# Score products of two head groups in row groups of TensorE, and two small products over all rows, in a two-layer hybrid mixer on one core

## The chip, the cores and the metric

The kernel runs on one core of a Trainium2 chip. The metric is the device time of one execution in microseconds (us); the time before is the median of three runs.

## The reference

One inference step of a backbone with two layers. There are 256 context tokens and 1024 latent tokens, 1280 rows of 1024 features. A layer normalises and modulates the tokens, projects them with `w_in` (1024 x 4400), runs three groups of heads side by side, and projects their gated result back with `w_out`:

- A, mLSTM: 4 heads of 128, exponential input gates with a running maximum m as stabiliser, a matrix state per head. The divisor of a token is `max(|den|, exp(-m))`.
- B, retention: 4 heads of 64 with a fixed decay per head, and a rotation of q and k on the latent tokens.
- C, gated linear attention: 4 heads with keys of 32 and values of 64, and a decay per key feature that comes out of a rank-16 product: `log_a = log_sigmoid(clr @ gla_w2 + gla_b2) / 16`.

Every group runs one scan forward and one backward over the tokens and adds the two; context tokens scan only themselves, latent scans start from cached states. In chunk form a group computes, per chunk, `scores = q k^T` times a decay, `scores @ v`, and the product of q with the state at the chunk's edge. The outputs are both normalised token arrays and the final context states.

## The kernel before, in words

Tokens are worked on in 10 chunks of 128 (chunks 0 and 1 are the context). The projections (`mm_fm`, L438, and `mm_tm`, L450) split both operands in two parts and take three products of 24 accumulating matmuls into one of two PSUM banks `pj`; everything else in PSUM goes through a ring `mx` of six banks. SBUF has 12 large tiles `f`, taken and given back, and rings of smaller ones (`rw`, 8 tiles of 512 columns, among them).

The order of the instructions on each engine is not written out. The program states every step, `ORDER` names the order of the steps of a layer, which gives their priority, and a planner that simulates all engines while the program is built lays the instructions of each engine in a row. A projection's matmuls get a priority lower by `LATE` (`late()`, L137), so that they fill what the mixers leave free on TensorE. Once laid, the order is fixed: an instruction that waits holds all behind it on its engine.

The steps that the change touches:

- **Gate rows** (`mlstm_rows`, L539). Forward heads are on partitions 0-3, backward heads on 32-35. A tile `TR` of 128 partitions collects gate rows in four quadrants. Ten transposes of `TR` (L590) and one copy per bank (L591) make the columns `ccol`. The row tile `m` becomes exp(-m) on ScalarE (L585); ten further transposes, of 36 rows (L595), and two copies a bank (L597) make the columns `ecol`.
- **Decays** (`decays`, L621). For each pair p of heads one matmul per block of tokens (L645), with the weights `w2[:, p, :]` on 64 partitions and the gate tile `G[0:64, ...]`.
- **C scores** (`group_c`, L804 to L832). Tiles `q[p]`, `k[p]` hold pair p: forward rows of its two heads on partitions 0-63, backward rows on 64-127, 32 rows per head and direction. For every two chunks GpSimd (L810) and ScalarE (L811) make copies of the queries in which one head of each direction is zeroed, and per chunk four matmuls over 64 rows with 256 columns (L819) put forward scores in one bank and backward scores in another. VectorE masks the forward scores into `PT` (L822) and overwrites the later half with the backward ones (L823). The output bank takes the state product (L827) and four score products (L830), and goes to `head_out` (L603).
- **B scores** (`group_b`, L1026 to L1038). For every two chunks eight matmuls over 64 rows with 128 columns (L1034), the heads on partitions 0-63 into one bank, those on 64-127 into the other; VectorE multiplies by the decay matrices (L1038).

In the trace every matmul in plain float32 (these all are) has two records, each with its weight load; transposes and the projections' matmuls have one.

Of the kernel before, what the change touches and what calls it, by code (L numbers as in the profile page):

```python
# [10 lines left out]
F32 = mybir.dt.float32  # L11
# [4 lines left out]
ALU = mybir.AluOpType  # L16
# [11 lines left out]
# the steps of layer() of either layer, in the order of their priority  # L28
# [11 lines left out]
# columns of w_in  # L40
# [13 lines left out]
def constants():  # L54
# [21 lines left out]
    # two-dimensional axial rotary angles of the latent grid  # L76
# [12 lines left out]
def hybrid_step(ctx: ExitStack, tc: tile.TileContext, A, O):  # L89
# [7 lines left out]
    class Ring:  # L97
        """n fixed tiles, handed out in turn; a tile may be used until its turn comes again"""
# [9 lines left out]
    class Arena:  # L108
        """fixed tiles [P, 1290], taken and given back; the one given back longest ago goes first"""
# [23 lines left out]
    def v3(t, n):  # L133
        """[P, a * n] as [P, a, n]"""
        return t.rearrange("p (a n) -> p a n", n=n)

    def late():  # L137
# [11 lines left out]
    heads_of = cp.tile([P, 2], F32, name="heads_of")  # L149
    for i in range(4):  # L150
        h = slice(32 * i, 32 * i + 32)
        pool.memset(heads_of[h, 0:1], 1.0 - i % 2)
        pool.memset(heads_of[h, 1:2], float(i % 2))
# [6 lines left out]
    # tau, as the decays of both directions take it  # L160
# [8 lines left out]
    # vectors as columns  # L169
# [21 lines left out]
    # half of headnorm_g, for silu through tanh  # L191
# [7 lines left out]
    def log_sigmoid(x, u, w):  # L199
        """x <- log(sigmoid(x)), with log1p(u) = ln(w) - ((w - 1) - u) for w = fl(1 + u); u, w scratch"""  # L200
# [33 lines left out]
    # small per-layer values that live long  # L234
# [12 lines left out]
    # scratch in DRAM  # L247
# [22 lines left out]
    def ada(l, c0, n, t, k):  # L270
        """loads k tiles k .. of n columns of w_ada into t; the tiles as views"""
# [5 lines left out]
    def modulation_pe(l, c0, n, units):  # L277
        """n columns on TensorE, a unit [P, k tiles * n] a step"""
# [15 lines left out]
    def modulation_dve(l, c0, n, acc, units):  # L294
        """n columns on VectorE, a unit [P, k tiles * n] a step; acc: two tiles [P, n]"""
# [24 lines left out]
    def background():  # L320
        """the next of the modulations that later stages need; its end comes with the next call"""
# [29 lines left out]
    def load_x(b):  # L351
        """tokens of block b, over their rms"""
# [26 lines left out]
    def norm_h(l, b, xn):  # L379
        """tokens over their rms, to modulated feature tiles, split"""  # L380
# [20 lines left out]
    # ---------------------------------------------------------------- weights  # L401
# [9 lines left out]
    def w_fm(src, c0):  # L411
        """128 columns of a weight matrix, split, [P, KT, 128]"""
# [1023 lines left out]
```

## Time and profile before

| what | value |
|---|---|
| time, median of 3 runs (lowest, highest) | 1673.07 us (1667.36, 1677.04) |
| span of the profiled execution, first to last instruction | 1660.9 us |
| the profiled execution's own time | not printed apart from its span |
| mean granted clock of TensorE | 0.987 |
| TensorE busy | 1591.4 us (96%) |
| VectorE, ScalarE, GpSimd busy | 1006.1 (61%), 614.1 (37%), 153.2 (9%) us |
| DMA | 167.43 MB, 101 GB/s |

"Busy" of an engine is the time in which at least one of its instructions is under way. PE is TensorE's matmuls, PEld its weight loads, DVE is VectorE, ACT ScalarE, POOL GpSimd, SP the engine whose queue issues most DMAs. The run's median is 12.2 us above the span of the profiled execution.

### The profile page before, as it was taken

What the parts mean: (1) busy time and instruction counts of PE and PEld (TensorE: products, weight loads), DVE (VectorE), ACT (ScalarE), POOL (GpSimd) and SP (SyncE); (2) the same over time, 40 slices, a digit from 0 to 9 for tenths busy, and PEclk for the clock granted to TensorE, in tenths of its full rate; (3) what the DMA queues carried; (4) which work ended last, traced back from release to release, by engine and by line L of the source; (5) the groups of instructions that cost most, each with busy time, mean ns of one, the idle gap of its engine ahead of it and who ended that gap; (6) DMA issues with size and microseconds to landing.
All of it is one profiled execution on the core that took longest, in us unless ns stands there. A gap on an engine that the chain in (4) does not pass through costs nothing.

```text
span 1660.9 us, 28470 instructions
## 1 busy us (share of the span) xinstructions
PE 1591.4 (96%) x10834; PEld 1429.1 (86%) x10834; DVE 1006.1 (61%) x2550; ACT 614.1 (37%) x1603; POOL 153.2 (9%) x242
## 2 busy tenths in 40 slices
PE   5898999999999999999999899999999999999997
PEld 1797879888989998889999787899988989888997
DVE  5766664768679855864364677454537633456545
ACT  2735424434112324342265453244411223434323
POOL 0200121001001101000011012100001100000001
PEclk8999999999999999999999999999999999999999
DMA  7411323544324533551141031333233132435203
GB/s 267 128 39 29 89 58 97 148 139 121 115 79 132 159 111 108 178 186 56 27 169 39 17 86 40 113 83 93 61 99 101 54 98 71 137 100 183 77 14 130
DMA packets 169312, 167.43 MB, mean 101 GB/s; under 512 B 19084, under 2 KB 144940, under 8 KB 169164
## 3 DMA queue, kind: packets, MB, share of 16 engines
q1 hardware_dynamic: 168992, 165.45, 32.8%
q8 instruction: 87, 1.43, 0.3%
q14 instruction: 61, 0.50, 0.1%
q10 hardware_dynamic: 172, 0.05, 0.0%
HBM read 129.49 MB, written 27.85 MB: 95 GB/s over the span
## 4 chain that ended last, share of the span: by engine, by line
PE 77%; DMA 8%; DVE 8%; ACT 3%; issue 2%; SPq 1%; POOL 0%; POOLq 0%; DVEq 0%; ACTq 0%
PE pj L446 31%; PE pj L458 25%; PE pj L526 3%; DMA rw<-rrow 2%; PE mx L1164 2%; DMA f<-in_w_ada_dram 2%; PE mx L819 2%; PE mx L1166 2%; PE mx L1113 2%; DVE f L496 1%; DMA wk<-yd 1%; PE mx L1155 1%; PE mx L1059 1%; PE mx L1034 1%; PE mx L991 1%
## 5 line engine op out<-in xcount | busy, mean ns | idle before, releaser
L446 PE MATMUL pj<-hA,hi 128*128 128x256 f32 (+1 forms) x1408 | 369.0, 344 | 0.1
L458 PE MATMUL pj<-hi,hA 128*128 128x256 f32 x1728 | 345.2, 287 | 5.9 <-ACT f L465 2.3
L458 PEld LDWEIGHTS pj<-hi,hA 128*128 128x128 f32 x1728 | 275.9, 190 | 10.2 <-ACT f L465 3.2
L446 PEld LDWEIGHTS pj<-hA,hi 128*128 128x128 f32 x1408 | 241.8, 189 | 30.6 <-issue 2.3
L458 PE MATMUL pj<-hi,hB 128*128 128x256 f32 x1152 | 249.1, 289 | 7.5 <-ACT f L1079 5.1
L446 PE MATMUL pj<-hA,lo 128*128 128x256 f32 (+1 forms) x704 | 238.2, 343 | 0.5 <-DVE lo L408 0.5
L458 PE MATMUL pj<-lo,hA 128*128 128x256 f32 x864 | 237.5, 286 | 0.0
L446 PE MATMUL pj<-hB,hi 128*128 128x512 f32 x704 | 234.3, 402 | 3.3 <-DVE wk L1197 1.3
L458 PEld LDWEIGHTS pj<-hi,hB 128*128 128x128 f32 x1152 | 194.2, 193 | 10.2 <-ACT f L1079 5.5
L408 DVE TENSOR_TENSOR lo<-raw,hi 128x256 fp32r<-128x256 f32 (+2 forms) x194 | 119.3, 627 | 95.3 <-ACT hi L407 83.5
L458 PE MATMUL pj<-lo,hB 128*128 128x256 f32 x576 | 165.9, 289 | 0.0
L458 PEld LDWEIGHTS pj<-lo,hA 128*128 128x128 f32 x864 | 159.9, 190 | 0.0
L446 PEld LDWEIGHTS pj<-hB,hi 128*128 128x128 f32 x704 | 129.5, 189 | 34.8 <-issue 4.1
L407 ACT CAST hi<-raw 128x256 fp32r<-128x256 f32 (+2 forms) x194 | 107.6, 566 | 138.0 <-PE pj L446 104.5
L446 PEld LDWEIGHTS pj<-hA,lo 128*128 128x128 f32 x704 | 132.5, 189 | 16.2 <-issue 1.0
L446 PE MATMUL pj<-hB,lo 128*128 128x512 f32 x352 | 140.5, 400 | 0.0
L458 PEld LDWEIGHTS pj<-lo,hB 128*128 128x128 f32 x576 | 110.7, 193 | 0.4 <-issue 0.3
L303 DVE SCALAR_TENSOR_TENSOR f<-f,sc 128x256 f32<-128x256 f32 x224 | 95.9, 479 | 15.2 <-DMA f<-in_w_ada_dram 15.2
L344 ACT ACTIVATE rw<-f 128x256 bf16<-128x256 f32 (+1 forms) x90 | 43.4, 484 | 116.1 <-DVE f L1334 105.5
L465 ACT COPY f<-pj 128x256 f32<-128x256 f32 (+2 forms) x142 | 48.4, 391 | 97.2 <-PE pj L458 48.2
L1148 DVE SCALAR_TENSOR_TENSOR rw<-rw,ccol,cst 128x128 f32<-128x128 f32 x160 | 46.7, 347 | 58.0 <-DMA rw<-rrow 57.9
L446 PEld LDWEIGHTS pj<-hB,lo 128*128 128x128 f32 x352 | 66.3, 188 | 15.3 <-issue 1.3
(283 smaller groups left out, 2566.9 us busy)
## 6 DMA issues: line engine op xcount, KB each, us to landing
raw<-in_w_in_dram SPq DMA_DIRECT2D x64, 512.0 KB
f<-in_w_ada_dram SPq DMA_DIRECT2D x32, 384.0 KB
wk<-yd SPq DMA_DIRECT2D x48, 256.0 KB
rw<-rrow SPq DMA_DIRECT2D x40, 256.0 KB
rw<-wrow SPq DMA_DIRECT2D x40, 256.0 KB
f<-in_w_ada_dram SPq DMA_DIRECT2D x16, 512.0 KB
f<-in_x_sample_dram SPq DMA_DIRECT2D x16, 512.0 KB
raw<-in_w_out_dram SPq DMA_DIRECT2D x32, 256.0 KB
```

What stands on the lines that cost most here:

```text
L303: dve.scalar_tensor_tensor(acc[v], w, scv[:, k, v:v + 1], acc[v], ALU.mult, ALU.add)
L344: act.activation(rw().bitcast(BF16)[:, 0:x.shape[1]], x, AF.Square, accum_out=out)
L407: act.copy(hi[:, e], raw[:, e])
L408: dve.tensor_tensor(lo[:, e], raw[:, e], hi[:, e].bitcast(F32), ALU.subtract)
L446: pe.matmul(ps[:, :n], lhsT=w[wi][:, k, :], rhs=hblk(xi, k, b), start=(i == 0), stop=(i == 23))
L458: pe.matmul(pv[:, u, :], lhsT=hchunk(xi, k, c), rhs=w[e // 4][wi][:, e % 4, :], start=(i == 0), stop=(i == 23))
L465: act.copy(out, ps)
L526: pe.matmul(ps, lhsT=hchunk(xi, k, c), rhs=w[k // 3][wi][:, k % 3, :], start=(i == 0), stop=(i == 23))
L819: pe.matmul(sc[d][:, 256 * p:256 * p + 256], lhsT=k[p][h, s], rhs=qm[p][h, :, u, :], start=True, stop=True)
L1113: pe.matmul(U[d], lhsT=ks[:, d * P:(d + 1) * P], rhs=v[:, c, :], start=True, stop=True)
L1148: dve.scalar_tensor_tensor(r4[:, d, e, :], r4[:, d, e, :], ccol[:, c0 + e, d, hd:hd + 1], negm[d], ALU.add, ALU.min)
L1164: pe.matmul(po[:, d, :], lhsT=r4[:, d, e, :], rhs=v[:, c, :], start=True, stop=not inter)
```

## The change

Four edits, and one helper for two of them. (All comments and docstrings are dropped as well; the constant `heads_of` goes.)

The helper `run(*banks)` takes the matmuls issued inside it, raises their priority by `LATE // 4`, makes the first of them wait for the last use of each of the banks by every engine but TensorE and SP, and chains each matmul to the one before it, so that the planner puts nothing in between.

```
+    @contextmanager
+    def run(*banks):
+        uses, n = last_uses(*banks), len(nc.cur_bb.bb.instructions)
+        with tc.high_priority(offset=LATE // 4):
+            yield
+        mms = nc.cur_bb.bb.instructions[n:]
+        for name in uses:
+            tc.add_manual_dep(mms[0], name, ...Sync...)
+        for a, b in zip(mms, mms[1:]):
+            tc.add_manual_dep(b, a.name, ...NoSync...)
```

Gate rows: exp(-m) of both directions is copied by two DMAs to rows 4-7 and 36-39 of `TR`, and comes out of the same transposes.

```
         act.activation(m, m, AF.Exp, scale=-1.0)
+        for d in range(2):
+            sync.dma_start(TR[32 * d + 4:32 * d + 8, :], m[32 * d:32 * d + 4, :])
...
-            ps = mx()
-            for j in range(n):
-                pe.transpose(ps[:, j * P:j * P + R], m[:, ...], ident[0:R, 0:R])
-            for d in range(2):
-                dve.tensor_copy(ecol[:, c0:c0 + n, d, :], ...)
+            dve.tensor_copy(ecol[:, c0:c0 + n, :, :], pv[:, :, 0:2, 4:8])
```

Decays: the weights take all 128 partitions (zeros but for the same rows), and so does the gate tile.

```
-        w2 = v3(sta(), P)[0:64]
+        w2 = v3(sta(), P)
...
-                pe.matmul(ps[:, :n], lhsT=w2[:, p, :], rhs=G[0:64, t0:t0 + n], ...)
+                pe.matmul(ps[:, :n], lhsT=w2[:, p, :], rhs=G[:, t0:t0 + n], ...)
```

C scores: no masked copies; for every two chunks sixteen matmuls over 32 rows with 128 columns, one per head and direction, in four banks by row group, and in one run. The VectorE passes and the output products are as many as before.

```
-            qm = []
-            for p in range(2):
-                t = rw()
-                x = q[p][:, c0 * P:(c0 + 2) * P]
-                pool.tensor_scalar(t[:, 0:256], x, heads_of[:, 0:1], None, ALU.mult)
-                act.activation(t[:, 256:512], x, AF.Copy, scale=heads_of[:, 1:2])
-                qm.append(...)
+            sc = [mx() for g in range(4)]
+            with run(*sc):
+                for u in range(2):
+                    s = slice((c0 + u) * P, (c0 + u + 1) * P)
+                    for p in range(2):
+                        for g in range(4):
+                            r = slice(32 * g, 32 * g + 32)
+                            pe.matmul(v3(sc[g], P)[:, 2 * u + p, :], lhsT=k[p][r, s], rhs=q[p][r, s],
+                                      start=True, stop=True, tile_position=(32 * g, 0))
+            PT = [v3(rw(), P) for t in range(2)]
+            for t in range(2):
+                dve.tensor_tensor(PT[t], v3(sc[t], P), m2..., ALU.mult)
+                dve.copy_predicated(PT[t], later..., v3(sc[2 + t], P))
             for u in range(2):
                 c = c0 + u
...
-                        pe.matmul(po[:, e], lhsT=PT[:, 2 * p + t, :], ...)
+                        pe.matmul(po[:, e], lhsT=PT[t][:, 2 * u + p, :], ...)
```

B scores: the same eight matmuls, inside `with run(*sc):`.

## Rows read from the trace of the kernel before

**Rows 1.** The page, engines (busy us, share, instructions) and the chain that ended last:
```profile
PE 1591.4 (96%) x10834; PEld 1429.1 (86%) x10834; DVE 1006.1 (61%) x2550; ACT 614.1 (37%) x1603; POOL 153.2 (9%) x242
...
PE 77%; DMA 8%; DVE 8%; ACT 3%; issue 2%; SPq 1%; POOL 0%; POOLq 0%; DVEq 0%; ACTq 0%
```

**Rows 2.** Windows (length; PE, PEld, DVE, ACT, POOL busy; clock): C and B of layer 0:
```profile
204.00:245.00 41.00, 41.00 (x198) 28.02 (x198) 28.89 (x74) 10.60 (x26) 10.41 (x12) 1.00 0.18 51
...
470.00:512.00 42.00, 42.00 (x310) 35.83 (x309) 34.68 (x111) 5.78 (x15) 5.04 (x5) 1.00 0.22 62
```

**Rows 3.** Groups by line and shape (busy us, mean ns), PE alone:
```profile
L819 PE MATMUL mx<-rw,f 64*128 64x256 f32 x160 | 35.7, 406 | 0.0
...
L1034 PE MATMUL mx<-f,f 64*128 64x128 f32 x160 | 18.2, 296 | 0.0
...
L645 PE MATMUL mx<-f,sta 64*128 64x512 f32 x16 | 8.2, 615 | 0.0
```

**Rows 4.** Timeline (start, length), PE, from 204.29, one run of C scores:
```profile
204.29 0.40 PE L446 MATMUL pj<-hB,lo 128*128 128x512 f32 x1
204.53 0.40 PE L446 MATMUL pj<-hB,hi 128*128 128x512 f32 x1
204.85 1.13 PE L819 MATMUL mx<-rw,f 64*128 64x256 f32 x4
205.91 0.71 PE L777 MATMUL mx<-f,sm 128*128 128x128 f32 x4
```

**Rows 5.** Timeline, PE: other runs of L819 and L1034, with first and last:
```profile
215.67 1.14 PE L819 MATMUL mx<-rw,f 64*128 64x256 f32 x8
...
1046.88 0.70 PE L819 MATMUL mx<-rw,f 64*128 64x256 f32 x2
...
473.36 0.93 PE L1034 MATMUL mx<-f,f 64*128 64x128 f32 x6
...
491.66 1.16 PE L1034 MATMUL mx<-f,f 64*128 64x128 f32 x16
...
1302.05 1.71 PE L1034 MATMUL mx<-f,f 64*128 64x128 f32 x16
```

**Rows 6.** Timeline, PE: the transposes of exp(-m), layer 0 and layer 1:
```profile
127.20 0.39 PE L446 MATMUL pj<-hA,hi 128*128 128x256 f32 x2
131.30 0.81 PE L595 MATMUL mx<-cst,f 36*128 36x36 f32 x10 [3.71 <-ACT f L585]
132.04 0.39 PE L446 MATMUL pj<-hA,lo 128*128 128x256 f32 x1
...
937.39 0.81 PE L595 MATMUL mx<-cst,f 36*128 36x36 f32 x10 [3.49 <-ACT f L585]
```

**Rows 7.** Windows behind that wait, layer 0 (clock is the third number from the end):
```profile
131.00:135.00 4.00, 3.70 (x26) 3.66 (x27) 1.55 (x9) 2.68 (x3) 0.00 (x0) 0.70 0.07 10
135.00:139.00 4.00, 4.00 (x17) 2.47 (x17) 0.00 (x0) 1.84 (x4) 0.11 (x1) 0.87 0.04 10
```

**Rows 8.** Timeline, SP's queue, POOL and PE between 133 and 152 us:
```profile
133.06 0.29 SPq L581 DMA_DIRECT2D wrow<-f  x1
...
135.28 0.11 POOL L642 MEMSET f<- 64x10 f32 x1 [47.20 <-DMA wrow<-f]
...
138.31 1.31 PE L590 MATMUL mx<-cst,f 128*128 128x128 f32 x10
...
151.48 3.84 SPq L414 DMA_DIRECT2D raw<-in_w_in_dram  x2
```

**Rows 9.** Line L819: VectorE's longest entry for idle time before it (us, times):
```profile
  DVE ti L610: 1.0, 3
```

**Rows 10.** Groups by line and shape: VectorE and GpSimd around the C scores:
```profile
L810 POOL TENSOR_SCALAR rw<-f,heads_of 128x256 f32<-128x256 f32 x20 | 23.6, 1191 | 78.4 <-DVE f L733 40.8 <-PE mx L819 37.3 <-POOL ti L611 0.2
L823 DVE COPY_PREDICATED rw<-later,mx 128x512 f32<-128x512 uint8 x20 | 14.5, 726 | 0.4 <-PE mx L819 0.2
L822 DVE TENSOR_TENSOR rw<-mx,masks 128x512 f32<-128x512 f32 x20 | 13.7, 685 | 9.9 <-PE mx L830 9.8
```

More of the change, by code (lines that the diff above doesn't have):

```diff
@@ L1 @@
-from contextlib import ExitStack
+from contextlib import ExitStack, contextmanager
 from itertools import chain
@@ L135, in v3, with last_uses @@
         return t.rearrange("p (a n) -> p a n", n=n)
+    def last_uses(*tiles):
+        names = {t.tensor.name for t in tiles}
+        found = {}
+        for ins in reversed(nc.cur_bb.bb.instructions):
+            if len(found) == 3 * len(names):
+                break
+            if ins.engine in (mybir.EngineType.PE, mybir.EngineType.SP):
+                continue
+            for ap in chain(ins.ins, ins.outs):
+                if hasattr(ap, "bass_ap") and ap.bass_ap.tensor.name in names:
+                    found.setdefault((ins.engine, ap.bass_ap.tensor.name), ins.name)
+        return sorted(set(found.values()))
+    @contextmanager
[5 more added lines that the diff above has]
+        for name in uses:
+            tc.add_manual_dep(mms[0], name, mybir.DependencyInfo(mybir.DependencyClass.Sync,
+                                                                 mybir.DependencyReason.DATA), reason="run")
+        for a, b in zip(mms, mms[1:]):
+            tc.add_manual_dep(b, a.name, mybir.DependencyInfo(mybir.DependencyClass.NoSync,
+                                                              mybir.DependencyReason.DATA), reason="run")
     def late():
@@ L148, in hybrid_step @@
     negm = [cst[:, K_MF:K_MF + P], cst[:, K_MB:K_MB + P]]
[L149 to L153, printed above, removed]
     masks = cp.tile([P, 256], BF16, name="masks")
@@ L644, in decays @@
                 ps = mx()
-                pe.matmul(ps[:, :n], lhsT=w2[:, p, :], rhs=G[0:64, t0:t0 + n], start=True, stop=True)
+                pe.matmul(ps[:, :n], lhsT=w2[:, p, :], rhs=G[:, t0:t0 + n], start=True, stop=True)
                 if general:
@@ L804, in group_c @@
         for c0 in range(0, NCH, 2):
-            qm = []
-            for p in range(2):
-                t = rw()
-                x = q[p][:, c0 * P:(c0 + 2) * P]
-                pool.tensor_scalar(t[:, 0:256], x, heads_of[:, 0:1], None, ALU.mult)
-                act.activation(t[:, 256:512], x, AF.Copy, scale=heads_of[:, 1:2])
-                qm.append(t.rearrange("p (t u i) -> p t u i", t=2, i=P))
+            sc = [mx() for g in range(4)]
[9 more added lines that the diff above has]
+            for t in range(2):
+                dve.tensor_tensor(PT[t], v3(sc[t], P), m2.unsqueeze(1).to_broadcast([P, 4, P]), ALU.mult)
+                dve.copy_predicated(PT[t], later.unsqueeze(1).to_broadcast([P, 4, P]), v3(sc[2 + t], P))
             for u in range(2):
@@ L815, in group_c @@
                 s = slice(c * P, (c + 1) * P)
-                sc = [mx() for d in range(2)]
-                for p in range(2):
-                    for d, h in enumerate(half):
-                        pe.matmul(sc[d][:, 256 * p:256 * p + 256], lhsT=k[p][h, s], rhs=qm[p][h, :, u, :],
-                                  start=True, stop=True)
-                PT = v3(rw(), P)
-                dve.tensor_tensor(PT, v3(sc[0], P), m2.unsqueeze(1).to_broadcast([P, 4, P]), ALU.mult)
-                dve.copy_predicated(PT, later.unsqueeze(1).to_broadcast([P, 4, P]), v3(sc[1], P))
                 bank = mx()
@@ L829, in group_c @@
                         e = slice(64 * t, 64 * t + 64)
-                        pe.matmul(po[:, e], lhsT=PT[:, 2 * p + t, :], rhs=v3(vt[p], 129)[:, c, e],
+                        pe.matmul(po[:, e], lhsT=PT[t][:, 2 * u + p, :], rhs=v3(vt[p], 129)[:, c, e],
                                   start=False, stop=(t == 1))
@@ L1026, in group_b @@
         for c0 in range(0, NCH, 2):
-            sc = [mx().rearrange("p (u r i) -> p u r i", u=2, i=P) for t in range(2)]
-            for u in range(2):
-                s = slice((c0 + u) * P, (c0 + u + 1) * P)
-                for r in range(2):
-                    for t in range(2):
-                        e = slice(64 * t, 64 * t + 64)
-                        pe.matmul(sc[t][:, u, r, :], lhsT=k[r][e, s], rhs=q[r][e, s], start=True, stop=True)
+            sc, v4 = [mx() for t in range(2)], lambda t: t.rearrange("p (u r i) -> p u r i", u=2, i=P)
+            with run(*sc):
+                for u in range(2):
+                    s = slice((c0 + u) * P, (c0 + u + 1) * P)
+                    for r in range(2):
+                        for t in range(2):
+                            e = slice(64 * t, 64 * t + 64)
+                            pe.matmul(v4(sc[t])[:, u, r, :], lhsT=k[r][e, s], rhs=q[r][e, s], start=True, stop=True)
+            sc = [v4(x) for x in sc]
             PT = [rw().rearrange("p (u r i) -> p u r i", u=2, i=P) for t in range(2)]
@@ L1058, in group_b @@
                     for t in range(2):
-                        pe.matmul(o[:, 64 * t:64 * t + 64], lhsT=PT[t][:, u, r, :], rhs=vv[r][:, c, 64 * t:64 * t + 64],
-                                  start=False, stop=(t == 1))
+                        pe.matmul(o[:, 64 * t:64 * t + 64], lhsT=PT[t][:, u, r, :],
+                                  rhs=vv[r][:, c, 64 * t:64 * t + 64], start=False, stop=(t == 1))
                 head_out(bank, 4, c)
```

6 lines of the change are left out of this document (2 added, 4 removed).

## The prediction

> **What bounds the kernel now.** I read the page's engine line and chain first. TensorE is busy 1591 us of 1661, and 77% of the chain that ended last is TensorE's own work [rows 1]: the reader is to see one engine that is nearly never free, with VectorE at 61% and ScalarE at 37% beside it. Then the windows over the stages that the change touches: in C and in B of layer 0 TensorE is busy for 41 of 41 and 42 of 42 us [rows 2], because the projections fill whatever the mixers leave. In such a stage nobody waits for the scores alone. What they take of TensorE is taken from the projections, so a microsecond less of TensorE is a microsecond less of the whole, as long as projections are at hand. VectorE, with 29 of 41 us in C and 35 of 42 us in B, is the next in line, and it is not full.
>
> Then the timeline, because a group's busy time does not show what a change of shape costs. Projection matmuls over 128 rows follow each other 0.24 us apart (204.29 to 204.53). The next instruction, a score over 64 rows, comes 0.32 us later, 0.09 late. Its four records take 1.06 us to the next 128-row product, and the four records of that one last 0.71 us, where a last record of 0.28 and three steps of 0.11 make 0.61 [rows 4]. So such a run costs its row's length and about 0.12 us more: 1.13 + 0.12 = 1.25 us. A run of two records has 0.70 [rows 5], so a record of 256 columns is (1.13 - 0.70) / 2 = 0.215, four are 0.86, and the other 0.39 is the change of the row count, there and back. The same holds for B: sixteen records cost 1.16 + 0.12 = 1.28, that is eight steps of 0.11 and 0.40.
>
> That last number shows the second thing: sixteen records, eight on each half of the rows, took eight steps. Both halves ran at once [rows 5]. In C eight records took 1.14 us, as long as four records elsewhere. But where a run holds one half alone, or the second half's bank is late, they go one by one: the sixteen records at 1302.05 took 1.71 [rows 5]. A run of two still costs 0.82.
>
> **The change, part by part.**
>
> C scores. Before: 160 records, busy 35.7 us [rows 3], in 35 runs of 2 to 10 records, of which rows 4 and 5 show one, a long one and the last: 35.7 + 35 x 0.12 = 39.9 us. After: 5 runs a layer, 10 in all, each of 16 matmuls, 32 records of 128 columns, eight in each of four row groups. No row of before has four row groups. The bounds: all four at once, eight steps of 0.11 and the change of 0.40, 1.28 us a run; one after the other, 32 x 0.11 + 0.40 = 3.92. The nearest row is B's run of sixteen: two groups, eight deep, 1.28 [rows 5]. Nothing there got slower for having two groups, so I take 1.28: 12.8 us. Gain 27.1 us; with one after the other 0.7.
>
> The Trainium skill ("TensorE: Matmul & The Clock Gate", Part 3, the table of measured speedups) gives 3.07 times for four row groups of 32 rows, not 4. By it a run would be 3.52 / 3.07 + 0.40 = 1.55 us (an estimate from that page) and the gain 24.4. No run of before has four groups; for two, the trace shows the full factor of two, so the sum keeps 1.28.
>
> B scores. Before: 18.2 us busy [rows 3] in 24 runs, first and last in rows 5: 18.2 + 24 x 0.12 = 21.1 us. After: 10 runs of sixteen records, 12.8 us by the row at 491.66. Gain 8.3. If the halves don't overlap (the row at 1302.05, 1.83 with its 0.12) it is 2.8.
>
> Decays. The columns streamed stay the same, all over 128 rows now, so six excursions of 0.39 go: 2.3 us (24 records; the larger form in rows 3). A full-row product of this shape stands nowhere in the trace; 0 if its records were longer by as much as is saved.
>
> Gate rows. The 36-row transposes took 131.30 to 132.04, 0.74, and about 0.10 behind them [rows 6]: 1.7 us for two layers. They are also where TensorE stood 3.71 and 3.49 us for exp(-m), with projections right behind them. And after these 3.7 idle us the granted clock was at its lower level, 1.2 GHz, for a while: 0.70 and 0.87 on the mean of two windows of 4 us [rows 7], that is 0.30 x 4 + 0.13 x 4 = 1.7 us lost a layer. All together 7.2 + 3.4 = 10.6 us, if nothing takes its place. The bound below is 0: the wait may move. The transposes of TR now wait for a DMA behind exp(-m). That was done by 131.3; a small DMA of the same rows goes from its issue at 133.06 to its reader at 135.28, 2.2 us [rows 8]; so TR is ready at some 133.5. TR's transposes stood at 138.31 [rows 8], 6.3 us behind the 132.04 of rows 6, or 4.6 without the 1.7 lost to the clock. Without the stall, at 127.6, TensorE would come to them at 132.2 and wait 1.3 instead of 3.7. So I take half of the 10.6: 5.3. The two DMAs themselves are of 4 rows each; on SP's queue no load of weights follows before 151.48 [rows 8], so two issues of 0.3 us hold up nothing. The copies to ecol halve, on VectorE, which did not set the pace.
>
> Masked copies of the queries. 23.6 us of GpSimd (L810) go [rows 10] and twenty ScalarE passes. They were beside TensorE's work; cost and gain 0, but for the two `rw` tiles a step that they held.
>
> The new wait. The first product of a run waits for all its banks at once, four of six in C, and whatever is laid behind it on TensorE (projections among it) waits with it. Before, the waits of C's scores on VectorE were single, the longest entry 1.0 us in three times [rows 9]. Below: 0, where the run is laid late enough. Above: every run comes early by the passes that empty its banks, two of 0.69 and two of 0.73, 2.8 us [rows 10], 20 x 2.8 = 56. The nearest rows are the small waits of rows 9, so I take 0.2 us a run: 4 us lost.
>
> Sum: 27.1 + 8.3 + 2.3 + 1.7 + 5.3 - 4 = 40.7 us. The span of 1660.9 becomes 1620.2. The median of the runs lies 12.2 us above that span, and I keep this distance: 1673.07 - 40.7 = 1632 us.
>
> **The rivals.**
>
> 1. *Issue becomes the bound in the runs of C.* For: the only short records that follow each other without another limit in sight, the 36-column transposes, come (0.81 - 0.23) / 9 = 0.064 us apart [rows 6], and a run of 32 at that pace takes 2.05 + 0.40 = 2.45 us instead of 1.28. Then 11.7 us less is gained: 1644 us. Two groups at a time instead of four (2.16 a run) would give much the same, 1641. Against: in the run at 491.66 records came (1.16 - 0.28) / 16 = 0.055 apart [rows 5], so they were queued already when it began, and there was no sign of a limit. The Trainium skill (same page, Part 1, "Wait - 56ns, not 53.3ns?") names about 62 ns of sequencer time per matmul where instructions are decoded in software; the 0.064 of the transposes agrees with it, the 0.055 shows that a queue can hide it for sixteen.
>
> 2. *The row groups don't overlap at all*, the change doesn't do what it says in C. For: at 1302.05 sixteen records over both halves went nearly one by one [rows 5]. Against: the overlap in the rows at 215.67 and 491.66. Gain 0.7 in C: 26.4 less, 1659 us.
>
> 3. *The runs hold TensorE*, the slower side. Place: the first product of each run. Price: up to 2.8 us for each of 20 runs, which is 56 us against a gain of 44.7 before waits; 1673 + 56 - 44.7 = 1684 us. It decides from 44.7 / 20 = 2.2 us a run. For: the order is fixed beforehand from a simulation, and the stall of 3.7 us in rows 6 shows that it can be early by that much; VectorE is busy for 70 to 83% of these stages [rows 2]. Against: a stall sets TensorE back to the pace of the others, so the next run no longer comes early; before, three such waits took 1.0 us together [rows 9]. To be paid twenty times VectorE would have to be the slower one all along, which it is not.
>
> 4. *More than forecast*: the whole 10.6 us at the gate rows and no new waits: 40.7 + 5.3 + 4 = 50, 1623 us. Tiles of `rw` that come free sooner may add a little.
>
> **How the numbers follow.** The forecast has 0.5 (about 1624 to 1640), issue or pairs 0.2, no overlap 0.08, the held engine 0.07, more than forecast 0.15. The order on all engines is laid anew, which no row prices; I widen both ends for it by some 8 us: 1615 to 1660, which leaves out the held engine and some of the far ends. A measurement of this kernel cannot tell less than about 0.5% (8.4 us) from no change: faster is below 1664.7. Forecast, rival 1 and rival 4 are faster, rival 2 mostly: 0.88; same 0.07 out of rivals 2 and 3; slower 0.05 out of rival 3.
>
> **What would show it.** C: ten rows of 32 records of at most 1.3 us at the new score line, with starts of four records a few ns apart; 2.3 us would be rival 1, 3.8 rival 2. B: ten rows of 16 at 1.16. Decays: no gap beside L645's successor. Gate rows: no 36-row transposes, and in front of TR's transposes an idle time below 3.7 us or none, with ScalarE or a DMA as its releaser. Idle time before the first record of a run, summed over 20, of 4 us or less; 40 would be rival 3. TensorE's busy time falls by about 36 us and stays at 96% of the span. The forecast is wrong if the span falls by less than 25 us though the score rows have the predicted lengths: then projections were not at hand where time came free.

## The result, and the profile after

| | median us (lowest, highest) | ratio to before, 95% interval |
|---|---|---|
| before, run beside it | 1670.21 (1664.76, 1677.04) | |
| after | 1688.62 (1686.15, 1691.05) | 1.0112 [1.0073, 1.0150] |

The change made the kernel slower by 1.1%; 1632 us was forecast, with 1615 to 1660 as the range. The runs of one kernel spread over up to 19 us, so small differences between two profiled executions are not read here.

The page of the kernel after, engine line and chain (the work that ended last, followed back from wait to wait), to be held against [rows 1]:

```profile
span 1689.2 us, 28682 instructions
PE 1578.0 (93%) x10974; PEld 1430.1 (85%) x10974; DVE 1005.3 (60%) x2544; ACT 607.1 (36%) x1585; POOL 127.8 (8%) x214
...
PE 66%; DVE 14%; DMA 12%; ACT 3%; issue 2%; SPq 1%; POOL 0%; DVEq 0%; POOLq 0%; ACTq 0%
```

TensorE has less work, 1578.0 us busy instead of 1591.4, but the span grew by 28.3. (The medians differ by 18.4: the execution of the kernel before that was profiled was one of its quicker ones, which makes up some 10 us of the 28.3 and bears on the next figures too.) The time in which it does nothing (span less busy) went from 69.5 to 111.2 us: +41.7 - 13.4 = +28.3. The granted clock fell from 0.987 to 0.969. With two levels, full (2.4 GHz) and half (1.2 GHz), that is 2 x 0.013 x 1660.9 = 43 us at half speed before and 2 x 0.031 x 1689.2 = 105 us after. Work done in those 62 us more takes up to twice as long, so up to 31 us went there: busy time fell by 13, not by the 36 forecast. TensorE's part of the chain went from 77% to 66%; VectorE and DMA took it over.

Yet the edited products became as short as forecast. Groups by line and shape of the kernel after (busy us, mean ns | idle before them), against [rows 3], and a stretch of its timeline, against [rows 4]:

```profile
L834 PE MATMUL mx<-f,f 32*128 32x128 f32 x320 | 11.7, 283 | 0.5 <-DVE rw L839 0.5
L1054 PE MATMUL mx<-f,f 64*128 64x128 f32 x160 | 11.6, 285 | 0.7 <-DVE f L1020 0.7
L666 PE MATMUL mx<-f,sta 128*128 128x512 f32 x16 | 7.8, 591 | 0.0
L615 PE MATMUL mx<-cst,f 128*128 128x128 f32 x20 | 3.6, 348 | 4.5 <-DMA f<-f 4.5
```

```profile
205.66 0.28 PE L469 MATMUL pj<-hA,hi 128*128 128x256 f32 x1
205.87 1.17 PE L834 MATMUL mx<-f,f 32*128 32x128 f32 x32
206.97 0.71 PE L846 MATMUL mx<-f,f 128*128 128x128 f32 x4
```

C's scores: 35.7 us busy became 11.7, a run takes 1.17 + 0.12 = 1.29 us where 1.28 was forecast. B's: 18.2 became 11.6. The idle time in front of the runs, the new wait for all banks, is 0.5 + 0.7 = 1.2 us in all twenty. So the loss is not at the score products. It is in the waits of other lines. Two of the largest are seen in the timeline of TensorE at the gate rows of layer 0 and of layer 1:

```profile
138.85 2.37 PE L615 MATMUL mx<-cst,f 128*128 128x128 f32 x10 [4.46 <-DMA f<-f]
...
959.84 0.79 PE L481 MATMUL pj<-hi,hA 128*128 128x256 f32 x2 [8.27 <-ACT f L488]
```

and the windows (columns as in [rows 2]) around the second, with the clock third from the end:

```profile
952.00:956.00 4.00, 0.00 (x0) 0.00 (x0) 3.97 (x5) 0.00 (x0) 0.00 (x0) 0.70 0.31 93
956.00:960.00 4.00, 0.16 (x1) 0.16 (x1) 3.55 (x9) 3.29 (x6) 0.11 (x1) 0.50 0.09 12
960.00:964.00 4.00, 4.00 (x20) 4.00 (x21) 0.33 (x2) 3.95 (x8) 0.00 (x0) 0.52 0.16 25
```

TensorE stands for 8.3 us, the clock goes to half while it stands, and when work is there again it is done at half speed for four more microseconds. This stall is paid twice.

### The profile page after: what moved, and what is told of

Read it like the earlier page. It is cut to its first block, busy times and chain, and to the rows that moved or that the text cites. A ratio compares the mean times of both kernels' runs of the same rounds, so it can differ in the third digit from the quotient of the medians.

```text
span 1689.2 us, 28682 instructions
## 1 busy us (share of the span) xinstructions
PE 1578.0 (93%) x10974; PEld 1430.1 (85%) x10974; DVE 1005.3 (60%) x2544; ACT 607.1 (36%) x1585; POOL 127.8 (8%) x214
## 4 chain that ended last, share of the span: by engine, by line
PE 66%; DVE 14%; DMA 12%; ACT 3%; issue 2%; SPq 1%; POOL 0%; DVEq 0%; POOLq 0%; ACTq 0%
PE pj L469 26%; PE pj L481 22%; DMA f<-in_w_ada_dram 4%; DMA rw<-rrow 3%; PE pj L549 3%; DVE f L326 2%; DMA f<-f 2%; PE mx L1185 2%; PE mx L1134 2%; PE mx L1187 1%; DMA wk<-yd 1%; DVE f L519 1%; DVE lo L431 1%; PE pj L306 1%; PE mx L1080 1%
## 5 line engine op out<-in xcount | busy, mean ns | idle before, releaser
L469 PE MATMUL pj<-hA,hi 128*128 128x512 f32 (+1 forms) x1408 | 372.8, 347 | 5.3 <-ACT f L488 3.6
L481 PEld LDWEIGHTS pj<-hi,hA 128*128 128x128 f32 x1728 | 280.2, 192 | 18.1 <-ACT f L488 10.1
L481 PE MATMUL pj<-hi,hB 128*128 128x256 f32 x1152 | 243.1, 290 | 10.9 <-ACT f L488 6.3
L481 PE MATMUL pj<-lo,hA 128*128 128x256 f32 x864 | 242.6, 287 | 0.0
L481 PEld LDWEIGHTS pj<-lo,hA 128*128 128x128 f32 x864 | 163.7, 192 | 0.3 <-issue 0.2
L1132 ACT ACTIVATE sm<-mx,ccol 128x128 f32<-128x128 f32 x144 | 49.7, 372 | 74.7 <-PE mx L1134 54.3
```

The costliest lines, as they stand in the source:

```text
L469: pe.matmul(ps[:, :n], lhsT=w[wi][:, k, :], rhs=hblk(xi, k, b), start=(i == 0), stop=(i == 23))
L481: pe.matmul(pv[:, u, :], lhsT=hchunk(xi, k, c), rhs=w[e // 4][wi][:, e % 4, :], start=(i == 0), stop=(i == 23))
L1132: act.activation(ks[:, d * P:(d + 1) * P], pk, AF.Copy, scale=ccol[:, c, 2 + d, hd:hd + 1])
```

## The experiments

"Idle" is the span of the profiled execution less TensorE's busy time; "clock" its mean granted clock. Both are of one execution each. Ratios are to runs of the kernel before on the same chip; for the kernel before idle is 69.5 us and the clock 0.987.

| kernel | median us | ratio, 95% interval | idle us | clock |
|---|---|---|---|---|
| e1 gate rows alone | 1681.28 | 1.0076 [1.0047, 1.0104] | 82.1 | 0.983 |
| e2 B's runs alone | 1669.36 | 0.9999 [0.9976, 1.0021] | 77.6 | 0.986 |
| e3 C alone, in runs | 1682.00 | 1.0086 [1.0060, 1.0113] | 89.2 | 0.971 |
| e4 two loads exchanged | 1669.65 | 0.9999 [0.9976, 1.0022] | 67.6 | 0.988 |
| e5 C without the run | 1663.68 | 0.9976 [0.9952, 1.0001] | 75.1 | 0.983 |
| e6 C's run by row group | 1675.03 | 1.0038 [1.0020, 1.0057] | 82.9 | 0.978 |
| e7 exp(-m) on GpSimd | 2103.65 | 1.2620 [1.2569, 1.2671] | 504.6 | 0.885 |
| e8 all but the gate rows | 1679.90 | 1.0087 [1.0059, 1.0114] | 98.9 | 0.971 |
| e9 C's run, no priority | 1681.86 | 1.0097 [1.0069, 1.0126] | 90.9 | 0.975 |
| e10 gate rows, exp(-m) last | 1670.88 | 1.0022 [1.0003, 1.0040] | 77.8 | 0.983 |
| e11 ecol behind ccol | 1676.43 | 1.0053 [1.0028, 1.0078] | 73.2 | 0.982 |
| e12 e5, decays, e11 | 1673.99 | 1.0037 [1.0016, 1.0058] | 75.4 | 0.975 |
| e13 C's run, no wait | 1686.34 | 1.0108 [1.0066, 1.0151] | 92.4 | 0.975 |
| e14 C's run, masks by chunk | 1675.03 | 1.0045 [1.0023, 1.0068] | 91.1 | 0.974 |
| e15 C without run, B, decays | 1672.09 | 1.0027 [1.0003, 1.0052] | 81.7 | 0.978 |
| e16 e15 and e10 | 1679.30 | 1.0055 [1.0029, 1.0081] | 87.4 | 0.973 |
| e17 two steps exchanged | 1680.12 | 1.0082 [1.0059, 1.0105] | 78.1 | 0.982 |
| e18 e5 and decays | 1662.80 | 0.9968 [0.9952, 0.9985] | 71.2 | 0.979 |

**Which edit costs.** Each part of the change alone on the kernel before, and one kernel with nothing changed but the order in which two small loads are issued. Three theories stood: the new order of all engines as such ('order'), exp(-m) in the way of evacuations on ScalarE ('gate rows'), the packed runs that bring TensorE early to its next wait ('runs').

e1, the gate rows alone (the diff of the gate rows, nothing else):

> The kernel before with the gate-row edit alone (exp(-m) by two DMAs into TR, no 36-row transposes). Theory 'order' (every edit saves its TensorE time, but the planner lays another order and the stalls are those of that order, whichever edit set it off): TensorE's own work falls by 2 us, the time may land anywhere from -10 to +20 us against before, and the stalls stand all over the program, not at TR's transposes alone. Theory 'gate rows' (exp(-m) now goes ahead of projection evacuations on ScalarE and holds TensorE): slower by 10 us or more, with the 8 us stall of layer 1 before TR's transposes there again, and most of the new stalls within mlstm_rows. Theory 'runs' (the packed runs make TensorE arrive early): within 5 us of before or faster.

e2, B alone:

```
+            with run(*sc):
                 ... the eight products of B's scores
```

> The kernel before with B's scores in runs, nothing else. All theories: the 10 runs take about 1.28 us each where 24 runs took 21.1 us together, 7 to 8 us of TensorE less. Theory 'gate rows': faster by 5 to 10 us. Theory 'order': the order behind B of layer 0 is laid anew, and the time lies between -12 and +15 us, not at -8. Theory 'runs': stalls before or right behind the ten runs, 5 to 15 us in all.

e3, C alone:

```
+            with run(*sc):
+                ... the sixteen products of C's scores, by row groups
```

> The kernel before with C's scores over 32 rows in four row groups and in runs, nothing else. All theories: the 10 runs cost about 14 us where 35 runs cost 40, 26 us of TensorE less. Theory 'gate rows': faster by 20 to 26 us. Theory 'runs': no faster than before, with the added stalls inside the two C stages. Theory 'order': gain between 0 and 26 us, stalls added outside the C stages too.

e4, the null case:

```
-            for t, row in ((v3(rb, 256), rrow), (wb, wrow)):
+            for t, row in ((wb, wrow), (v3(rb, 256), rrow)):
```

> The kernel before with the two loads of each step of head_a (rrow's and wrow's rows) issued in the other order: same instructions, same work, another laid order from about a fifth of the program on. Theory 'order': the time moves by more than 0.5% (8 us) with TensorE's own work unchanged, the idle time of TensorE by as much. Theories 'gate rows' and 'runs': same time as before within 0.5%.

Gate rows +12 us, C +13, B 0, the null case 0. e1 has the two stalls of the gate rows again, 8.27 and 4.4 us. With the decays, at most -2, the parts make +23 where the whole change has +18. So the loss has two places, and two edits that were forecast to gain 5 and 27 us lost 12 and 13. The null case seemed to do away with 'order'; e17, below, takes that back. e8 agrees:

> The whole change without the gate-row edit: C's and B's runs and the decays. If the edits add up (C +13, B 0, decays -2 on 1669): 1678 to 1682 us, and the gate rows are worth the rest of the 1688. If they work on each other (C's early TensorE is slowed again elsewhere): anywhere from 1665 to 1690; below 1670 would say that the gate rows are what turned the gain into a loss.

1679.9 was measured, inside the additive forecast of 1678 to 1682.

**The gate rows.** ScalarE of the kernel after in layer 1, then SP's queue in layer 0 (DMA issues; the second column is the length of the issue):

```profile
956.70 1.28 ACT L608 ACT_TABLE_LOAD   x1 [14.89 <-DVE ti L592]
958.00 1.27 ACT L608 ACTIVATE f<-f 36x1280 f32<-36x1280 f32 x1
959.17 1.15 ACT L488 COPY f<-pj 128x256 f32<-128x256 f32 x4
```

```profile
133.85 0.71 SPq L610 DMA_DIRECT2D f<-f  x1
134.97 0.26 SPq L604 DMA_DIRECT2D wrow<-f  x1
...
136.02 0.24 SPq L605 DMA_DIRECT2D arow<-ti  x1
136.31 0.64 SPq L610 DMA_DIRECT2D f<-f  x1
```

exp(-m) (L608) now belongs to the columns that come first, and the planner laid it on ScalarE ahead of four evacuations of projection banks (L488). It waits 14.89 us for VectorE's chain, the evacuations stand behind it though their banks are full, and TensorE waits for a bank. In layer 0 the second of the two DMAs is laid behind four others, which wait for exp(wa); it is issued 2.5 us after the first, and TensorE stands 4.46 us.

On top of e1, e7 takes exp(-m) off ScalarE; e10 leaves it there but behind exp(kw):

```
-        act.activation(m, m, AF.Exp, scale=-1.0)
+        pool.tensor_tensor(m, einv[0:R, :].to_broadcast([R, T]), m, ALU.pow)
```

> The gate-row edit alone, with exp(-m) computed on GpSimd as a power of 1/e instead of on ScalarE; nothing else changed. Theory 'ScalarE' (most of the 12 us that the gate-row edit costs is exp(-m) standing on ScalarE ahead of evacuations of projection banks, 8.3 us idle at 937 us and some 10 us at 1.2 GHz behind it): that stall goes, 1668 to 1673 us. Theory 'late' (the transposes of TR simply come before exp(-m) and its DMA are done, wherever it is computed): GpSimd is slower, by 1280 columns at 1.19 us per 256 some 6 us, against about 1.5; the stalls at the transposes grow by that in each layer, with the clock behind them: 1684 to 1695 us.

```
         act.activation(TR[64:100, :], kw, AF.Exp)
+        last = nc.cur_bb.bb.instructions[-1].name
         act.activation(m, m, AF.Exp, scale=-1.0)
+        tc.add_manual_dep(nc.cur_bb.bb.instructions[-1], last, ...NoSync...)
```

> The gate-row edit alone (1681 us), with one more dependency: exp(-m) stands behind exp(kw) on ScalarE, which puts it behind the four evacuations that it held up in layer 1. Theory 'ScalarE': the 8.3 us of idle TensorE at 937 us and most of the 10 us at 1.2 GHz after it go; the transposes of TR now wait for exp(kw), exp(-m) and the DMA in turn (1.3 + 2.2 us longer in layer 0): 8 us better than the edit alone, 1670 to 1675 us. Rival 'late' (what TensorE loses is the wait for the DMA, whatever stands on ScalarE): no better, 1680 to 1686 us.

e7 tells nothing: its price was wrong by far. The group row of that kernel:

```profile
L587 POOL TENSOR_TENSOR f<-einv,f 36x1280 f32<-36x1280 f32 x2 | 407.9, 203952 | 87.0 <-DVE ti L571 87.0
```

204 us for one power, where the 6 us came from a multiplication's row. The trace of the kernel before has powers of its own on GpSimd: 1.02 us for 4 columns and 0.54 for one, that is 0.16 us a column, which would have given 205. e10 came out as theory 'ScalarE' has it: 1670.9, 10 us better than e1. Its ScalarE and TensorE in layer 1:

```profile
938.95 1.20 ACT L465 COPY f<-pj 128x256 f32<-128x256 f32 x4 [9.46 <-PE pj L458]
...
952.23 1.27 ACT L586 ACTIVATE f<-f 36x1280 f32<-36x1280 f32 x1
```

```profile
956.90 2.37 PE L594 MATMUL mx<-cst,f 128*128 128x128 f32 x10 [5.61 <-DMA f<-f]
```

The evacuations go first, the 8.3 us are gone, and 5.6 us of waiting for the DMA of exp(-m) are left. What is left of that wait is longer than the 3.49 us that TensorE stood there in [rows 6]. In layer 0 the 4.4 us for the DMA are gone, and 4.2 us for an evacuation stand in their place.

e11 asks whether that old stall was worth its size, in the kernel before, by laying the 36-row transposes last:

```
+        # first all transposes of TR and the copies to ccol, then:
                 pe.transpose(ps[:, j * P:j * P + R], m[...], ident[0:R, 0:R])
+                tc.add_manual_dep(nc.cur_bb.bb.instructions[-1], last, ...NoSync...)
```

> The kernel before with one edit: the 36-row transposes of exp(-m) are laid behind the transposes of TR instead of ahead of them; no DMA, nothing folded. In the kernel before TensorE stood 3.7 and 3.5 us for exp(-m) there, with 3.4 us at 1.2 GHz after each. Theory 'worth its size' (the prediction priced this stall at up to 10.6 us): the stall goes, TR's transposes wait 1 to 2 us at most, 1658 to 1662 us. Rival 'given back' (TensorE only comes early to the next wait): 1666 to 1670 us, with a stall of 2 to 4 us at the transposes of TR or at the evacuations right behind.

It was given back, and more: 1676.4. The stall shrank from 3.7 to 2.7 us in layer 0 and from 3.5 to 1.0 in layer 1, but it now stands in front of TR's transposes, and at one line of the projections TensorE's waits for evacuations grew from 1.1 to 6.9 us. Windows of e11 and, in the second fence, of the kernel before:

```profile
132.00:146.00 14.00, 13.00 (x41) 9.58 (x41) 2.44 (x11) 3.21 (x5) 0.33 (x3) 0.51 0.17 44
```

```profile
132.00:146.00 14.00, 14.00 (x62) 9.98 (x60) 1.53 (x11) 7.07 (x12) 0.33 (x3) 0.88 0.03 6
```

After a shorter stall, with twenty transposes behind it instead of ten, the clock stayed at half for nearly the whole 14 us. That is 0.12 x 14 = 1.7 us lost to the clock before, and 0.49 x 14 = 6.9 in e11.

**C.** Why does a run of 1.29 us that hardly waits lose 13 us? e5 leaves the run away (`run` does nothing any more) and keeps the products, e6 keeps the run and makes its products slow, one row group after the other:

```
     def run(*banks):
-        uses, n = last_uses(*banks), len(nc.cur_bb.bb.instructions)
-        with tc.high_priority(offset=LATE // 4):
-            yield
-        ...
+        yield
```

> C's score products by row groups of 32 rows, without the run: no chain, no raised priority, no wait for all banks at once; B, the gate rows and the decays as before. Theory 'run' (C's loss of 13 us comes from holding the sixteen products together: VectorE gets four banks at once and the output products behind them wait): the stalls of the C stages (16 us more than before in the run alone) go, and what the packed products save, less the changes of row count where the run is broken up, is left: 1645 to 1660 us. Theory 'early' (TensorE is through its score products sooner than the order was laid for, arrives early at products that wait for VectorE, and its granted clock falls to 1.2 GHz after each such stall): no better than with the run, 1678 to 1690 us. Theory 'data flow' (four banks and both masks ahead of any output product): likewise about 1682, with the stalls at the output products of C themselves.

```
-                for u in range(2):
-                    for p in range(2):
-                        for g in range(4):
+                for g in range(4):
+                    for u in range(2):
+                        for p in range(2):
```

> C's score products by row groups in one run, but laid one row group after the other, so that no two groups can run at once: 32 records of 0.11 us and 0.4 are 3.9 us a run instead of 1.35, 25 us more of TensorE in ten runs. Theory 'early': the 25 us are taken out of the stalls that the quick runs had, the time stays where it was with the quick run, 1677 to 1687 us, and the idle time and the time at 1.2 GHz fall. Rival (the stalls have nothing to do with how quick the products are; the new order costs what it costs): 25 us on top, 1700 to 1710 us.

The score groups of e3, e5 and e6:

```profile
L840 PE MATMUL mx<-f,f 32*128 32x128 f32 x320 | 13.3, 310 | 2.3 <-DVE ti L638 1.2 <-DVE rw L845 1.1
```

```profile
L830 PE MATMUL mx<-f,f 32*128 32x128 f32 x320 | 27.1, 300 | 1.8 <-DVE rw L834 1.6 <-DVE rw L835 0.2
```

```profile
L840 PE MATMUL mx<-f,f 32*128 32x128 f32 x320 | 28.2, 283 | 0.0
```

The quickest scores, 13.3 us, are in the slowest of the three kernels (1682); 28.2 us of the same products, in a run too, make 1675, and 27.1 us, broken up among projections, 1664. e6 was expected to add 25 us of TensorE; it added 14.9 (2.82 us a run, because the end of one row group still ran beside the start of the next), and the time fell by 7. 'Early' had said that it stays at 1677 to 1687, and 1675 is just below that; the rival said 1700 to 1710. Part of the time goes in the C stage of layer 0, windows of e3, e5 and e6:

```profile
204.00:245.00 41.00, 34.09 (x288) 28.35 (x286) 27.06 (x67) 6.71 (x16) 4.29 (x6) 0.85 0.20 51
```

```profile
204.00:245.00 41.00, 37.37 (x298) 30.64 (x297) 29.59 (x76) 7.80 (x20) 5.26 (x7) 1.00 0.27 67
```

```profile
204.00:245.00 41.00, 38.59 (x304) 33.39 (x302) 27.96 (x70) 7.33 (x20) 4.33 (x6) 1.00 0.13 36
```

Before, TensorE was busy for 41.00 of 41.00 at full clock [rows 2]. With the quick run it is idle for 6.9 us and at 0.85. Half of that, 3.4 us, is in front of C's own products: the longest is 2.0 us at an output product that waits for the second mask pass (L845). Behind it the clock is at half; a line of e3's timeline and a window:

```profile
217.85 0.43 PE L855 MATMUL mx<-f,rw 128*128 128x64 f32 x2 [2.03 <-DVE rw L845]
```

```profile
224.00:229.00 5.00, 5.00 (x14) 3.94 (x14) 1.35 (x4) 0.38 (x1) 1.44 (x2) 0.50 0.00 0
```

The other 3.5 us are the start of a stall at another place. Here is what it waits for, e3's VectorE and then TensorE:

```profile
240.69 0.17 DVE L638 TENSOR_SCALAR ti<-ti 128x4 f32<-128x4 f32 x1
244.04 1.14 DVE L1173 SCALAR_TENSOR_TENSOR rw<-rw,ccol,cst 128x128 f32<-128x128 f32 x4 [3.19 <-DMA rw<-rrow]
245.10 0.41 DVE L641 TENSOR_TENSOR sm<-mx,ti 128x256 f32<-128x256 f32 x1
```

```profile
240.34 1.17 PE L840 MATMUL mx<-f,f 32*128 32x128 f32 x32 [1.22 <-DVE ti L638]
245.66 0.66 PE L643 MATMUL mx<-cst,sm 128*128 128x128 f32 x2 [4.15 <-DVE sm L641]
```

`head_out`'s normalisation (L641) stands on VectorE behind a step of A (L1173) that waits 3.19 us for the load of a gate row. TensorE comes to `head_out`'s transposes (L643) meanwhile and stands 4.15 us, with the projections behind it. That wait of VectorE is not new. What is new is who waits with it. The lists of "idle until" at A's step (VectorE) and at `head_out`'s transposes (TensorE) in the kernel before:

```profile
  DMA rw<-rrow: 57.9, 34
...
  DVE sm L613: 0.6, 1
```

and in the kernel after:

```profile
  DMA rw<-rrow: 53.9, 35
...
  DVE sm L634: 11.4, 8
```

VectorE waits for these loads for some 55 us in either kernel, 34 or 35 times. At `head_out`'s transposes alone, TensorE stood once for 0.6 us before and eight times, 11.4 us together, after; in e3 it is 9.9 us in 5, in e5 4.1 in 4, in e6 7.5 in 5. Not all of it hangs on these loads: a wait of VectorE for one overlaps in time two of e3's five stalls (7.3 of the 9.9 us) and two of the eight after (5.6 of the 11.4).

Three further kernels take the run apart. e9 drops its priority, e13 its wait for all banks, e14 keeps it whole but masks the first chunk first, in passes of 256 columns:

```
-        with tc.high_priority(offset=LATE // 4):
-            yield
+        yield
```

> C by row groups in a run, with the chain and with the wait for all banks, but without the raised priority. Before is 1668, with the whole run 1682, without any run 1664. Theory 'priority' (the run costs 18 us because its products are pulled ahead of other work, and head_out's transposes then stand at VectorE): 1664 to 1670 us, and the stalls of 3 to 4 us at head_out's transposes go. Theory 'at once' (it is the sixteen products coming at once, so that VectorE gets four banks together and the output products and head_out come behind them): 1677 to 1684 us, with these stalls as they were.

```
-        for name in uses:
+        for name in ():
```

> C in a run with its chain and its priority, but the first product doesn't wait for all four banks; each product waits for its own bank alone. Before 1667, with the whole run 1682, without any run 1664. Theory 'banks' (the wait for all banks holds TensorE or pushes the run behind VectorE's last pass): 1664 to 1672 us. Theory 'at once' (what costs is that sixteen products and then four masks come in one piece): 1677 to 1684 us, with the stalls at head_out's transposes and at C's output products as in the whole run.

```
+            for u in range(2):
+                e = slice(2 * u, 2 * u + 2)
                 for t in range(2):
-                    dve.tensor_tensor(PT[t], v3(sc[t], P), ...)
-                    dve.copy_predicated(PT[t], ..., v3(sc[2 + t], P))
+                    dve.tensor_tensor(PT[t][:, e, :], v3(sc[t], P)[:, e, :], ...)
+                    dve.copy_predicated(PT[t][:, e, :], ..., v3(sc[2 + t], P)[:, e, :])
```

> C with the whole run, but the masks cut by chunk: eight passes of 256 columns instead of four of 512, those of the first chunk first, so that its output products wait for half of the masks and head_out's work on VectorE can go in between. It adds work: at 0.69 and 0.73 us per 512 columns, some 0.1 us a pass of fixed cost, 4 us of VectorE in all. Theory 'at once': the stalls of 2 to 4 us at C's output products and at head_out's transposes shrink, 1668 to 1676 us. Theory 'early' alone (TensorE is ahead of the order, wherever VectorE puts its passes): 1679 to 1686 us.

Neither priority (1681.9) nor wait (1686.3, with an interval that overlaps the run's) is the cause alone. Nor does the C stage of layer 0 decide the time: e13, the slowest of these, is about as busy there as e5, at full clock:

```profile
204.00:245.00 41.00, 38.96 (x309) 29.53 (x307) 28.64 (x74) 8.08 (x21) 4.29 (x6) 1.00 0.16 39
```

Cutting the masks gives 7 us, the time that 'at once' expected, but not by its way: the intervals of e3 and e14 overlap at their ends, and the stalls that were to shrink did not. At `head_out`'s transposes e14 has 11.6 us of idle time where e3 has 9.9, at C's output products 3.9 where e3 has 3.3. So the run costs 18 us against the same products without it, and by which of its parts these runs don't settle. What e3, e6, e9, e13 and e14 share and e5 lacks is the chain that holds the sixteen products together; the chain alone, without priority and wait, was not run.

**What a newly laid order costs.** e17 changes no instruction, it exchanges two neighbouring steps in each layer's order of priority:

```
-    "g v0 cq ck m d k1 C q0 k0 o0 a0 ...
+    "g v0 cq ck m d k1 C k0 q0 o0 a0 ...
-    "g cq v0 ck m q0 d C k0 k1 o0 z6 ...
+    "g cq v0 ck m q0 d C k1 k0 o0 z6 ...
```

> The kernel before with two neighbouring steps exchanged in the order of priority (the projections q0 and k0 of A in layer 0, k0 and k1 in layer 1): the same instructions in a newly laid order. Theory 'any new order' (the order of before is a lucky one, and edits of 5 to 10 us drown in what a new order brings): 1672 to 1685 us, with new stalls in stages that nobody touched. Rival (losses come from what the edits do): 1663 to 1671 us.

13 us slower, by the same two things: 78.1 us idle instead of 69.5, and a clock of 0.982 instead of 0.987. e4's new order had cost nothing, but it moved only some 320 of TensorE's 10834 records, where e17 moved some 890. So an order may cost anything from 0 to 13 us by itself, and a difference of that size between two kernels of this study can't be put down to the edit's own mechanism alone. Every edit but the decays' also lays a new order. What speaks against mere bad luck in C is that all seven kernels with its run (e3, e6, e8, e9, e13, e14 and the change itself) are slower than before, and e5 and e18 are not.

**Versions that should be faster.**

e12 (e5, the decays' change and e11's order), e15 (e5, B's run, the decays), e16 (e15 with e10's gate rows), e18 (e5 and the decays), with the edits shown above:

> Three edits together: C by row groups without the run (1664 alone), the decays over 128 rows (no more than 2.3 us by the changes of row count), and the transposes of exp(-m) laid behind those of TR. If they add up, with the last one worth its size: 1651 to 1657 us; if the last is given back: 1660 to 1664 us. Should a newly laid order bring stalls of its own, it is slower than either part.

> The change without its two causes of loss: C by row groups without the run, B in runs, decays over 128 rows, gate rows as before. By the single runs: C -4, B 0, decays at most -2: 1660 to 1665 us, against 1667 before. If edits that relieve TensorE are given back as stalls when they come together: 1666 to 1675 us.

> As the one before, with the gate rows folded into the transposes of TR and exp(-m) held behind exp(kw) on ScalarE. By the single runs the folded gate rows then cost 4 us: 1663 to 1670 us. If they come into the way of the other edits: above 1672 us.

> C by row groups without the run and the decays over 128 rows; the order of all engines is that of C without the run alone. C without the run measured -4.4 us, the decays lose up to six changes of row count at 0.39 us: 1659 to 1664 us. Should a saving on TensorE in an unchanged order be given back as waiting: 1663 to 1666 us, the time without the decays' change.

Savings don't add up: B's run, worth 0 alone, makes e18 9 us slower (e15); e10's gate rows add another 7 to that (e16); e11's order makes e18 11 us slower (e12). e18 alone is ahead of both kernels: 1662.8 us, ratio 0.9968 [0.9952, 0.9985]. That is 4 us of the 29.4 that the prediction gave to its two edits. Nearly all of it is e5's: e18 is laid as e5 on every engine, its interval overlaps e5's, and so a gain by the decays is not shown.

## Why the prediction was wrong

**The step that failed** is the first one: "a microsecond less of TensorE is a microsecond less of the whole, as long as projections are at hand." The windows of [rows 2] show TensorE busy all the time in C and in B, and I read that as a queue that is never empty. But the order on each engine is fixed beforehand. Projections fill the places where they were laid, not the places where time comes free. C and B were to gain 35.4 us; alone, C lost 13 and B gained nothing. B shows it plainest (e2): its products take 11.6 us instead of 18.2, TensorE is busy for 5.9 us less, and it is idle for 8.1 us more (69.5 to 77.6). Engine line and score group of e2, against [rows 1] and [rows 3]:

```profile
PE 1585.5 (95%) x10834; PEld 1424.5 (86%) x10834; DVE 1004.5 (60%) x2550; ACT 613.4 (37%) x1603; POOL 152.9 (9%) x242
...
L1062 PE MATMUL mx<-f,f 64*128 64x128 f32 x160 | 11.6, 285 | 0.2 <-DVE f L1029 0.2
```

The prediction had named this sign itself: score rows of the forecast length, and a span that falls by less than 25 us. That TensorE merely comes earlier to the same wait can be read at single stalls, as at 241.5 in e3. It isn't shown for the sum, because B's and C's edits also lay new orders, and e17 shows that a new order alone can cost as much.

**The sum, term by term.** C's products: right (12.9 by the prediction's own method, 12.8 forecast), and B's (12.8). Decays: the records got no longer, 7.8 us where they took 8.2, but that the 2.3 us were gained is not shown (e18). Waits in front of the runs: 4 us forecast, 1.2 measured. The gate rows: +5.3 and 1.7 forecast, -12 measured alone. There the prediction looked at ready times only ("TR is ready at some 133.5"; its transposes began at 138.85) and said that "two issues of 0.3 us hold up nothing" (they took 0.71 and 0.64). It did not ask what would hold them up, or what exp(-m) would: the second issue stands behind four others, and exp(-m), now needed earlier, went ahead of evacuations. What the sum had no term for: 42 us more of idle TensorE, nearly all in lines other than the scores, and 62 us more at half clock. The 3.7 us stall of [rows 6] with its clock in [rows 7] had shown both prices at one place; they had to be put on new stalls too, not only on the old one that was to go.

**The rivals.** Rival 3, "the runs hold TensorE", gave 1684 and so came near the time, but by luck, from a place that stayed empty: 1.2 us instead of 56. It fell as a mechanism; what took its place is TensorE standing at other products (the projections, `head_out`'s and TR's transposes), which hang on ScalarE, VectorE and DMA. Rival 1, issue as the bound: the 32 records took 1.17 us, some 0.03 apart; the 0.064 did not appear. Rival 2 fell with it: in the first run the records of the four row groups start 7 ns apart, and from the second four on, four come every 0.11 us, as forecast.

The Trainium skill gives 3.07 times for four row groups ("TensorE: Matmul & The Clock Gate", Part 3). The prediction put that figure on the 32 steps alone and got 1.55 us a run; 1.29 was measured, and here the measurement decides. Put on the whole run with its change of row count, the same figure would fit: the 3.92 us estimated for one group after the other, over 1.29, is 3.0. The trace does not contradict the page, whose row is for 512 columns.

**The range.** 8 us were added to both ends for the order that is laid anew. e17 shows that such an order alone may cost 13, and of the two neutral new orders (e4, e17) none was faster; 8 us to both sides was too little on the slow side. Nor is the upper end worked out: 8 us above rival 1 is 1652, above rival 2 1667, and 1660 is neither. But 13 us would not have helped either, for 1688.62 lies 28.6 above it: the main terms were wrong, not only the margin.

**The distance to the median.** The 12.2 us between the median and the profiled span were taken as fixed. The profiled execution of the kernel after took 1690.95 us, 1.75 above its span; before's profile was simply one of its quicker executions.

## What to carry to other kernels

In a kernel whose orders are fixed when it is built, a busy engine is not a bound by itself: ask at each edit which instruction comes next on that engine, what it waits for, and whether that is ready earlier too. Put the price of the lower clock on a stall that an edit may bring. Try neutral exchanges of two steps first, and more than one (here one moved the time by 0 and another by 13 us), because they tell how much of any later difference the order alone can make. Where something is made ready by a shorter way, look at what it will now stand in front of, on the queue that computes it and on the one that moves it.

## What the hardware showed unexpectedly

- Four row groups of 32 rows ran side by side: 32 records took 1.17 us, as long as B's sixteen in two groups (1.16). Laid one group after the other they took 2.82.
- GpSimd's power of 36 x 1280 elements took 204 us, ScalarE's exponential of the same tile 1.27.
- How long the clock stayed at half after a stall differed much, and what decides it is not shown: over 14 us the mean was 0.88 behind a stall of 3.7 us, with ten transposes of 36 rows and then projections, and 0.51 behind one of 2.7, with twenty transposes first. Behind e3's stall of 2.0 us, with C's own products next, it was still at half from 224 to 229.
